# A two-layer decoder trunk: triangular inverse on 64x64 blocks, threshold search on keys with a sign per row, and the second layer's first loads ahead of a loop

## The chip, the cores and the metric

The kernel runs on one core of a Trainium2 chip, as one program. The metric is the device time of one execution in microseconds (us), the median of several runs. TensorE is called PE below, with PEld for its weight loads; VectorE is DVE, ScalarE is ACT, GpSimd is POOL, and SyncE, whose queue issues most transfers, is SP.

## The reference

Two decoder layers run one after the other over 1024 tokens of width 1024. Each layer mixes tokens with four head groups (RWKV-7, stick-breaking attention, mLSTM, and a sparse attention DSA), and then runs a mixture of 32 experts. What matters here, cut down:

```python
# RWKV-7: a delta rule over time; the kernel works in chunks of 64 tokens,
# and within a chunk the rule becomes a triangular system (I - L) T = I
def step(state, inp):
    rt, wt, kt, vt, kkt, at = inp
    sa = jnp.einsum('bhvk,bhk->bhv', state, -kkt)
    state = (state * wt[:, :, None, :] + sa[..., None] * (kkt * at)[:, :, None, :]
             + vt[..., None] * kt[:, :, None, :])
    return state, jnp.einsum('bhvk,bhk->bhv', state, rt)

# DSA: each query keeps its 256 best keys
idx_score = jnp.where(adm, idx_score, -jnp.inf)
vals, sel = lax.top_k(idx_score, n_sel)

# experts: top 2 of 32, results added at the tokens' rows
x = x + gt2 * hier_moe(h, ...)
```

## The kernel before

**Stages.** Per layer: the normed input and the first columns of the input projection (the head: `head`, `hidden`, `proj_i`); a weave of the projection on PE with the search for the 256th best score of each row on DVE and ACT (`proj` and `select`, which calls `Dsa.search`); a weave of four streams (`rw.run()`, which is RWKV; `dsr()` and `rest()`, which are the attentions and mLSTM; `mods()`; `outs()`, the output projection), called stage 3 below; the routing; the experts, one after another, each with 12 pieces of 512 KB of weights read from HBM. After the experts `moe.overflow` runs a loop whose number of turns is read from memory; in layer 1 it turns no time in the profiled execution, in layer 2 once (3544 to 3597 us). A weave takes the streams' pieces by turns, and a scheduler then places each instruction in its engine's order, which is fixed when the program is built.

**RWKV.** `Rwkv.run` keeps up to three units alive; a unit is one pair of heads over 128 tokens, that is two chunks of 64 tokens in two heads. There are 16 units in a layer: five batches of three and one alone. A unit holds the tiles `ra`, `bkv`, `mp` and `tl`. In `unit` the inverse T of each chunk is built by doubling: a mask `lev` cuts a level out of the 64x64 triangle, and in five steps a product `pw` (PSUM pool `b`), its copy by ACT into `ra`, a product `pT` (PSUM pool `pj`) and an addition by DVE into `tl` double the size of the blocks that are done; T and its transpose are both kept. Before, the two chunks of a head stand on the diagonal of a 128x128 matrix whose other two quarters are zero, so each product is one 128x128x128 matmul per head. All matmuls here are float32, and each leaves two records in the trace.

**The search.** `Dsa.search` finds each row's threshold bit by bit, first 16 upper bits of the score as a bfloat16 key (`upper`), then 16 lower bits (`lower`). Six tiles of 128 rows, 384 to 1024 keys wide, form two groups of three that take turns; per bit and group one count runs on ACT (line 1022) and two on DVE (line 1024), and small DVE operations on a 128x3 tile then decide the bit.

**The queue at the layer boundary.** The second layer's first loads are issued by SP in program order behind the loop: eight pieces of `w_in` (`wr`), the norm's gain (`ng`), the modulation (`mod`), then the tokens' rows `x`, which the experts' last scatters into `xs` (POOL, line 1502) must have written.

Of the kernel before, what the change touches and what calls it, by code (L numbers as in the profile page):

```python
# [12 lines left out]
BF16 = mybir.dt.bfloat16  # L13
# [36 lines left out]
def const_table():  # L50
# [24 lines left out]
    lev = lambda b: (s // (2 * b) == t // (2 * b)) & (s % (2 * b) < b) & (t % (2 * b) >= b)  # L75
# [19 lines left out]
class K:  # L95


    def __init__(self, ctx, tc, nbig, nmed, consts_dram):
# [9 lines left out]
        t = self.big("lev", 768)  # L108
        self.nc.sync.dma_start(t, consts_dram[:, NCONST:NCONST + 768])
        self.lev = self.cp.tile([P, 768], BF16, name="levb")  # L110
# [134 lines left out]
class Rwkv:  # L245
# [109 lines left out]
    def unit(self, ct, hf, nb, own):  # L355
# [28 lines left out]
        ml, w1 = [two(w[:, 256 * i:256 * i + 256]) for i in range(2)], two(ra[:, 256:512])  # L384
        tt = w[:, 512:1024].rearrange("p (x h t) -> p x h t", x=2, h=2)
        l2 = mp[:, :, 0, :].unsqueeze(2).to_broadcast([P, 2, 2, 64])
        four = lambda x: x.rearrange("p h (c t) -> p h c t", c=2)
        lv = lambda i: k.lev[:, 128 * i:128 * i + 128].rearrange("p (c t) -> p c t", c=2).unsqueeze(1).to_broadcast([P, 2, 2, 64])
        V.tensor_tensor(four(tt[:, 1]), l2, lv(0), op=ALU.mult)
        V.tensor_tensor(tt[:, 1], tt[:, 1], k.c("ident").unsqueeze(1).to_broadcast([P, 2, P]), op=ALU.add)  # L390
        for i in range(2):
            G.tensor_tensor(four(ml[i]), l2, lv(i + 1), op=ALU.mult)

        def chunks(out, a, b):
# [10 lines left out]
        for i in range(5):  # L405
            last = i == 4
            pw = two(k.psum("b", 256))
            for h in range(2):
                k.mm(pw[:, h], ml[i % 2][:, h], tt[:, 0, h])
            k.act(w1, pw)  # L410
            if i < 3:
                G.tensor_tensor(four(ml[i % 2]), l2, lv(i + 3), op=ALU.mult)
            pT = k.psum("pj").rearrange("p (x h t) -> p x h t", x=2, h=2)
# [10 lines left out]
        chunks(pn, mp[:, :, 2, :], two(bkv[:, 2, :]))  # L424
# [82 lines left out]
    def run(self, width=3):  # L507
# [7 lines left out]
        free = [(k.med("ra"), k.med("bkv", 384), k.med("mp"), k.big("tl", 1024)) for _ in range(width)]  # L515
# [353 lines left out]
class Dsa:  # L869
# [122 lines left out]
    def search(self):  # L992
# [4 lines left out]

        k, nc = self.k, self.k.nc
# [4 lines left out]
        cnt, sg, tt, k1, ml, thr, half_n = (t[:, 6 * i:6 * i + 6] for i in range(7))  # L1003
# [10 lines left out]
        for j, i in enumerate(tiles):  # L1014
            V.memset(half_n[:, j:j + 1], width(i) / 2.0)

        def counts(keys, val, g):

            for j in range(3 * g, 3 * g + 3):
# [3 lines left out]
                else:  # L1023
                    V.tensor_scalar(junk[j % 3 - 1][:, :width(i)], keys[i], v, None, op0=ALU.is_ge, op1=ALU.add,  # L1024
# [1182 lines left out]
```

## Time and profile before

| | |
|---|---|
| median of 3 runs | 3617.0 us (3612.22 to 3620.91) |
| the profiled execution | 3611.5 us, span 3609.7 us |
| mean granted TensorE clock of it | 0.922 of full speed |
| PE, DVE, ACT, POOL busy | 88%, 77%, 53%, 25% of the span |
| stage 3, layer 1 and layer 2 | 445 to 1165 us and 2240 to 2895 us |
| experts, layer 1 and layer 2 | 1200 to 1812 us and 2927 to 3544 us |

The busy share of an engine is a mean over stages with different limits, so each stage has to be read by itself; a chain of waits says which work was late in it. The span is the time from the first to the last instruction, 1.8 us less than the execution's own time.

### The profile page before, as it was taken

How to read it: one execution, taken by the hardware profiler on the slowest of the kernel's cores; microseconds unless marked ns; L12 is line 12 of the kernel's file. 1: busy time of each engine (PE TensorE's matmuls, PEld its weight loads, DVE VectorE, ACT ScalarE, POOL GpSimd, SP SyncE). 2: the span in 40 equal slices, each digit the busy share in tenths (PEclk: the TensorE clock that was granted, in tenths of full speed). 3: DMA queues.
4: the chain of work that ended last, by engine and by line, in shares of the span. 5: the costliest groups of instructions: out<-in, count | busy, mean ns of one | idle time of the engine just before them, and what ended most of it. 6: DMA issues, size and time to landing. Idle time of an engine off the chain costs nothing.

```text
span 3609.7 us, 54562 instructions
## 1 busy us (share of the span) xinstructions
PE 3185.2 (88%) x18836; PEld 2491.4 (69%) x18848; DVE 2778.3 (77%) x5552; ACT 1928.5 (53%) x3324; POOL 900.9 (25%) x769
## 2 busy tenths in 40 slices
PE   6888989998888799999968888989888879999996
PEld 3876745576666677777758766767676667887775
DVE  4589854567776899999965898666677679999996
ACT  3456333334444567777753563542444456777774
POOL 3220110113322215522312201121332221353231
PEclk8988989999997899999989899989889879999998
DMA  5222365433434799999932233023343379999996
GB/s 199 77 86 88 107 217 203 162 128 106 135 115 149 276 366 386 381 381 382 385 114 66 85 94 105 29 71 122 106 141 121 128 257 371 381 381 382 384 382 225
DMA packets 373672, 746.63 MB, mean 207 GB/s; under 512 B 44234, under 2 KB 108384, under 8 KB 373392
## 3 DMA queue, kind: packets, MB, share of 16 engines
q1 hardware_dynamic: 346880, 672.03, 51.7%
q0 software_dynamic: 20256, 70.33, 7.5%
q8 instruction: 151, 2.47, 0.3%
q10 hardware_dynamic: 6256, 0.74, 0.1%
q14 instruction: 129, 1.06, 0.1%
HBM read 635.45 MB, written 107.53 MB: 206 GB/s over the span
## 4 chain that ended last, share of the span: by engine, by line
PE 47%; DVE 21%; DMA 18%; issue 7%; ACT 4%; POOL 2%; SPq 1%; ACTq 0%; DVEq 0%; POOLq 0%
PE pj L143 26%; PE b L143 14%; DMA wr<-in_moe_w_dram 11%; DVE dkey L1024 4%; PE a L143 3%; PE a L148 2%; DMA xs<-yo,si 2%; DVE wl L1535 2%; DVE e L589 1%; PE pj L148 1%; ACT wh L160 1%; PE b L148 1%; DVE h L1785 1%; DVE yo L1499 1%; DVE z L591 1%
## 5 line engine op out<-in xcount | busy, mean ns | idle before, releaser
L160 ACT ACTIVATE wh<-wr 128x1024 fp32r<-128x1024 f32 (+3 forms) x900 | 886.7, 1006 | 293.8 <-DMA wr<-in_moe_w_dram 111.5
L1535 DVE TENSOR_TENSOR wl<-wr,wh 128x1024 fp32r<-128x1024 f32 x792 | 935.5, 1220 | 55.9 <-ACT wh L160 45.4
L143 PE MATMUL pj<-wh,xh 128*128 128x512 f32 x1056 | 421.5, 400 | 11.2 <-ACT xh L160 9.2
L143 PE MATMUL pj<-wl,xh 128*128 128x512 f32 x1056 | 418.7, 403 | 13.7 <-DVE wl L1535 13.2
L143 PE MATMUL pj<-wh,xl 128*128 128x512 f32 x1056 | 419.8, 398 | 0.0
L143 PEld LDWEIGHTS pj<-wl,xh 128*128 128x128 f32 x1056 | 200.1, 189 | 81.2 <-DVE wl L1535 37.6
L143 PEld LDWEIGHTS pj<-wh,xh 128*128 128x128 f32 x1056 | 199.8, 190 | 58.1 <-ACT xh L160 11.8
L143 PEld LDWEIGHTS pj<-wh,xl 128*128 128x128 f32 x1056 | 200.4, 190 | 45.5 <-DVE xl L1547 1.0
L1431 POOL DMA_INDIRECT xg<-h2d,si x64 | 78.4, 1224 | 582.5 <-PE a L148 345.5
L143 PE MATMUL b<-wh,hh 128*128 128x512 f32 x528 | 210.5, 399 | 10.2 <-ACT wh L160 9.1
L143 PE MATMUL b<-wh,hl 128*128 128x512 f32 x528 | 208.1, 394 | 1.2 <-DVE hl L1547 1.2
L143 PE MATMUL pj<-hh,wh 128*128 128x512 f32 x480 | 196.6, 410 | 13.0 <-ACT wh L160 5.9
L143 PE MATMUL pj<-wh,hh 128*128 128x256 f32 (+2 forms) x640 | 187.8, 306 | 17.2 <-DVE stl L1977 11.0
L143 PE MATMUL pj<-hh,wl 128*128 128x512 f32 x480 | 195.3, 407 | 3.9 <-DVE wl L1860 3.9
L1502 POOL DMA_INDIRECT xs<-yo,si x32 | 164.1, 5127 | 134.0 <-DVE yo L1499 117.6
L143 PE MATMUL pj<-wh,hl 128*128 128x256 f32 (+2 forms) x640 | 192.9, 303 | 3.0 <-DVE hl L1837 2.8
L1502 POOL DMA_INDIRECT out_dram<-yo,si x32 | 160.9, 5027 | 134.1 <-DVE yo L1499 117.5
L143 PE MATMUL pj<-hl,wh 128*128 128x512 f32 x480 | 193.9, 404 | 0.0
L143 PE MATMUL pj<-wl,hh 128*128 128x256 f32 (+2 forms) x640 | 189.1, 298 | 2.7 <-POOL wl L1860 2.7
L143 PE MATMUL b<-wl,hh 128*128 128x512 f32 x528 | 174.7, 410 | 2.3 <-DVE wl L1535 2.1
L160 ACT ACTIVATE ra<-b 128x256 f32<-128x256 f32 x192 | 72.9, 383 | 187.8 <-PE b L143 185.1
L421 DVE TENSOR_TENSOR tl<-pj,tl 128x512 f32<-128x512 f32 x128 | 87.4, 686 | 80.7 <-PE pj L143 80.0
(524 smaller groups left out, 7725.7 us busy)
## 6 DMA issues: line engine op xcount, KB each, us to landing
wr<-in_moe_w_dram SPq DMA_DIRECT2D x792, 512.0 KB
aw<-in_ada_w_dram SPq DMA_DIRECT2D x96, 512.0 KB
wr<-in_w_in_dram SPq DMA_DIRECT2D x84, 256.0 KB
wo<-in_w_out_dram SPq DMA_DIRECT2D x48, 256.0 KB
xs<-xp SPq DMA_DIRECT2D x48, 256.0 KB
xp<-xs SPq DMA_DIRECT2D x48, 256.0 KB
out_dram<-xp SPq DMA_DIRECT2D x48, 256.0 KB
sk<-pt SPq DMA_DIRECT2D x32, 256.0 KB
```

What stands on the lines that cost most here:

```text
L143: return self.nc.tensor.matmul(out, lhsT, rhs, start=start, stop=stop, skip_group_check=True)
L148: return self.nc.tensor.transpose(out, in_, self.c("ident")[o:o + n, o:o + n])
L160: i = self.nc.scalar.activation(out, in_, f, **kw)
L421: V.tensor_tensor(tt, pT, tt, op=ALU.add)
L589: V.tensor_tensor_scan(e[:, :kl][:, ::-1], e[:, :kl][:, ::-1], e[:, :kl][:, ::-1], initial=0.0, op0=ALU.add, op1=ALU.bypass)
L591: V.tensor_tensor(z[:, :kl], z[:, :kl], e[:, :kl], op=ALU.subtract)
L1024: V.tensor_scalar(junk[j % 3 - 1][:, :width(i)], keys[i], v, None, op0=ALU.is_ge, op1=ALU.add, accum_out=cnt[:, j:j + 1])
L1431: i = self.k.nc.gpsimd.indirect_dma_start(out=xg, out_offset=None, in_=self.h2d, in_offset=bass.IndirectOffsetOnAxis(ap=gi.bitcast(U32), a ...
L1499: i = V.scalar_tensor_tensor(yo[:, ns], py[n], gate, gt2[:, ns], op0=ALU.mult, op1=ALU.mult)
L1502: k.nc.gpsimd.indirect_dma_start(out=self.xs, out_offset=bass.IndirectOffsetOnAxis(ap=si.bitcast(U32), axis=0), in_=yo, in_offset=None, co ...
L1535: i = nc.vector.tensor_tensor(wl, raw, wh.bitcast(F32), op=ALU.subtract)
L1785: V.scalar_tensor_tensor(hs[i], xs[i], ms[:, 2 + i:3 + i], s, op0=ALU.mult, op1=ALU.mult)
```

## The change

It has three parts. In `Rwkv.unit` the 128x128 matrices with two zero quarters become 64x64 blocks, one per chunk, so the work tile, the masks and the copies are half as wide, and each 128x128 matmul becomes two 64x64 ones. In `Dsa.search` the keys are multiplied by a sign `sg` per row as ACT casts them, the counts on DVE count what is below the threshold, and a limit `lim` per row takes the place of the conversions behind each count. In `run` and `head` the pieces of `w_in` of the second layer are fetched and split ahead of the overflow loop, and `head2` holds what stays behind it.

```diff
-        ml, w1 = [two(w[:, 256 * i:256 * i + 256]) for i in range(2)], two(ra[:, 256:512])
-        tt = w[:, 512:1024].rearrange("p (x h t) -> p x h t", x=2, h=2)
+        ml, w1 = [two(w[:, 128 * i:128 * i + 128]) for i in range(2)], two(ra[:, 256:384])
+        tt = w[:, 256:512].rearrange("p (x h t) -> p x h t", x=2, h=2)
...
+        def chunks(*jobs):
             for h in range(2):
-                for c in ch:
-                    k.mm(out[c, h], a[c, h], b[c, h])
+                for out, a, b in jobs:
+                    for c in ch:
+                        k.mm(out[c, h], a[c, h], b[c, h])
-        pT = two(k.psum("b", 256))
+        pT = two(k.psum("b", 128))
         for h in range(2):
-            k.tr(pT[:, h], tt[:, 1, h])
+            for c in ch:
+                k.mm(pT[c, h], tt[c, 1, h], k.c("rep64")[c])
...
-            for h in range(2):
-                k.mm(pw[:, h], ml[i % 2][:, h], tt[:, 0, h])
+            chunks((pw, ml[i % 2], tt[:, 0]))
...
-            for h in range(2):
-                if not last:
-                    k.mm(pT[:, 0, h], tt[:, 1, h], w1[:, h])
-                k.mm(pT[:, 1, h], w1[:, h], tt[:, 1, h])
+            chunks(*[(pT[:, 0], tt[:, 1], w1)] * (not last), (pT[:, 1], w1, tt[:, 1]))
...
-        for h in range(2):
-            k.mm(pu[:, h], tt[:, 1, h], rh[:, h].rearrange("p x c -> p (x c)"))
+        chunks((pu, tt[:, 1], two(ra[:, 0:256])))
...
-                    V.tensor_scalar(junk[j % 3 - 1][:, :width(i)], keys[i], v, None, op0=ALU.is_ge, op1=ALU.add,
+                    V.tensor_scalar(junk[j % 3 - 1][:, :width(i)], keys[i], v, None, op0=ALU.is_lt, op1=ALU.add,
...
-        for i in tiles:
-            k.act(key[i], half[i][:, :, 1])
...
+        for j, i in enumerate(tiles):
+            k.act(key[i], half[i][:, :, 1], scale=sg[:, j:j + 1])
...
-                fix(g)
-                yield
-                V.scalar_tensor_tensor(tt[:, s], cnt[:, s], 0.5 - TOPK, sg[:, s], op0=ALU.add, op1=ALU.mult)
-                yield
                 if bit > 15:
-                    V.tensor_scalar(k1[:, s], tt[:, s], 0.0, float(1 << bit), op0=ALU.is_ge, op1=ALU.mult)
+                    V.tensor_tensor(k1[:, s], cnt[:, s], lim[:, s], op=ALU.is_le)
                     yield
-                    V.tensor_tensor(m[:, s], m[:, s], k1[:, s], op=ALU.add)
+                    V.scalar_tensor_tensor(m[:, s], k1[:, s], float(1 << bit), m[:, s], op0=ALU.mult, op1=ALU.add)
...
+        if l + 1 < L_LAYERS:
+            self.head(l + 1)
         moe.overflow(gt2)
```

On PE, one step of one unit of the first batch in layer 1, before. `b` is the product `pw` or a copy, `pj` the product `pT`, `tl` and `ra` the unit's tiles; `pj<-aw,cz` belongs to `mods()`, `dz`, `dat` and `dsum` to `dsr()`.

```order
L143 MATMUL b_4858<-tl_4463 128x128 x2
L143 MATMUL b_4915<-tl_4455 128x128 x2
L143 MATMUL pj_4836<-aw_4837,cz 32x512 x2
L148 MATMUL pj_4846<-cst,dz_4802 128x128 x3
L143 MATMUL pj_4863<-ra_4460,tl_4463 128x128
L143 MATMUL pj_4863<-tl_4463,ra_4460 128x128
L143 MATMUL pj_4863<-ra_4460,tl_4463 128x128
L143 MATMUL pj_4863<-tl_4463,ra_4460 128x128
L143 MATMUL pj_4836<-aw_4839,cz 32x512 x2
L143 MATMUL b_4851<-dat_4845,dv_325 64x128
```

The same place in the changed kernel:

```order
L143 MATMUL b_4777<-tl_4346 64x64 x4
L143 MATMUL pj_4720<-aw_4721,cz 32x512 x2
L148 MATMUL pj_4730<-cst,dz_4697 128x128 x3
L143 MATMUL pj_4742<-ra_4339,tl_4342 64x64 x2
L143 MATMUL pj_4742<-tl_4342,ra_4339 64x64 x2
L143 MATMUL pj_4742<-ra_4339,tl_4342 64x64 x2
L143 MATMUL pj_4742<-tl_4342,ra_4339 64x64 x2
L143 MATMUL pj_4720<-aw_4723,cz 32x512 x2
L143 MATMUL b_4752<-dat_4729,dv_325 64x128
```

The two 128x128 matmuls of `pw` became four 64x64 ones and the four of `pT` eight, in the same neighbourhood: matmuls of other streams, on the whole array or on parts of another shape, stand between the groups as before.

On DVE, one upper bit of both groups of the search in layer 1, before: line 1058 makes the thresholds, 1024 counts, 1041 to 1070 decide.

```order
L1058 TENSOR_SCALAR dmi_2213<-dmi_2213 128x3
L1024 TENSOR_SCALAR dkey_2215,dth_2212<-dkey_2215,dmi_2213 128x768
L1024 TENSOR_SCALAR dkey_2216,dth_2212<-dkey_2215,dmi_2213 128x512
L1041 SCALAR_TENSOR_TENSOR dth_2212<-dth_2212 128x1
L1065 SCALAR_TENSOR_TENSOR dth_2212<-dth_2212 128x3
L1068 TENSOR_SCALAR dth_2212<-dth_2212 128x3
L1041 SCALAR_TENSOR_TENSOR dth_2212<-dth_2212 128x1
L1070 TENSOR_TENSOR dmi_2213<-dmi_2213,dth_2212 128x3
L1065 SCALAR_TENSOR_TENSOR dth_2212<-dth_2212 128x3
L1058 TENSOR_SCALAR dmi_2213<-dmi_2213 128x3
L1068 TENSOR_SCALAR dth_2212<-dth_2212 128x3
L1024 TENSOR_SCALAR dkey_2215,dth_2212<-dkey_2214,dmi_2213 128x640
```

In the changed kernel, where line 1056 makes the thresholds, 1022 counts, and 1062 and 1064 decide:

```order
L1056 TENSOR_SCALAR dmi_2213<-dmi_2213 128x3
L1022 TENSOR_SCALAR dkey_2215,dth_2212<-dkey_2215,dmi_2213 128x768
L1022 TENSOR_SCALAR dkey_2216,dth_2212<-dkey_2215,dmi_2213 128x512
L1062 TENSOR_TENSOR dth_2212<-dth_2212 128x3
L1064 SCALAR_TENSOR_TENSOR dmi_2213<-dth_2212,dmi_2213 128x3
L1056 TENSOR_SCALAR dmi_2213<-dmi_2213 128x3
L1022 TENSOR_SCALAR dkey_2215,dth_2212<-dkey_2214,dmi_2213 128x640
```

Per group and bit three small operations are left of five, and here they stand one behind another, where before those of the two groups alternated.

On POOL, at the end of layer 1's experts, in the changed kernel (before, the two scatters into `xs` stand next to each other, and the splits `wl` behind the loop):

```order
L1497 DMA xs_80<-yo_17233,si_11302 1152x1024
L1863 TENSOR_TENSOR wl_17309<-wr_17292,wh_17308 128x292
L1863 TENSOR_TENSOR wl_17313<-wr_17294,wh_17312 128x292
L1863 TENSOR_TENSOR wl_17317<-wr_17296,wh_17316 128x292
L1863 TENSOR_TENSOR wl_17321<-wr_17298,wh_17320 128x292
L1863 TENSOR_TENSOR wl_17325<-wr_17300,wh_17324 128x292
L1863 TENSOR_TENSOR wl_17329<-wr_17302,wh_17328 128x292
L1863 TENSOR_TENSOR wl_17333<-wr_17304,wh_17332 128x292
L1497 DMA xs_80<-yo_17288,si_11302 1152x1024
```

Seven of the eight splits moved in front of the last scatter. On SP, behind the loop, the changed kernel issues two pieces of `x` first, then `ng`, `mod` and the others; the eight `wr` stand ahead of the loop.

## Rows read from the trace of the kernel before

**Rows 1.** Windows by stage: projection and search, stage 3, experts.
```profile
core 0: us, PE busy (x) PEld busy (x) DVE busy (x) ACT busy (x) POOL busy (x), PEclk, DMA share, GB/s
200.00:445.00 245.00, 218.46 (x1046) 178.53 (x1046) 229.04 (x741) 130.51 (x237) 36.04 (x48) 0.91 0.32 98
445.00:1165.00 720.00, 636.32 (x4779) 446.95 (x4781) 445.83 (x949) 276.07 (x657) 156.05 (x199) 0.91 0.45 151
1200.00:1812.00 612.00, 591.17 (x2699) 470.65 (x2699) 564.80 (x631) 453.27 (x508) 196.85 (x59) 0.99 1.02 371
2240.00:2895.00 655.00, 571.55 (x4490) 446.34 (x4495) 443.77 (x947) 276.83 (x660) 157.14 (x195) 0.89 0.32 103
```

**Rows 2.** Chain of waits by line, stage 3 of layer 2.
```profile
by line: PE b L143 24.4%; PE pj L143 23.6%; PE a L143 8.2%; issue 5.8%; DVE e L589 3.7%; PE pj L148 3.2%; PE a L148 3.1%; DVE z L591 1.7%; DVE wol L2096 1.3%; DMA sk<-pt 1.2%; ACT e L160 1.1%; DMA wo<-in_w_out_dram 1.1%; DVE tl L421 1.0%; A
```

**Rows 3.** Windows of the twelve stretches with inverse steps, all tiles; columns as above.
```profile
871.00:920.00 49.00, 47.45 (x366) 39.98 (x366) 36.79 (x65) 22.16 (x55) 16.44 (x26) 1.00 0.38 131
...
2378.00:2449.00 71.00, 61.14 (x411) 48.74 (x414) 39.77 (x86) 22.03 (x60) 12.77 (x17) 0.83 0.14 43
...
sum 661.00, PE 585.42 PEld 458.66 DVE 440.24 ACT 264.07 POOL 167.32; mean PE 48.79 PEld 38.22 DVE 36.69 ACT 22.01 POOL 13.94
```

**Rows 4.** The same windows, instructions of tile tl alone.
```profile
sum 661.00, PE 287.12 PEld 250.74 DVE 101.55 ACT 11.53 POOL 72.67; mean PE 23.93 PEld 20.90 DVE 8.46 ACT 0.96 POOL 6.06
```

**Rows 5.** Timeline: start us, us, engine, line, operation; 128x128 matmuls of `pT`.
```profile
706.38 0.39 PE L143 MATMUL pj<-tl,ra 128*128 128x128 f32 x2
...
706.60 0.39 PE L143 MATMUL pj<-ra,tl 128*128 128x128 f32 x2
```

**Rows 6.** Timeline: chunk matmuls of 64x64 between 128x128 ones.
```profile
712.82 0.61 PE L143 MATMUL pj<-tl,ra 128*128 128x128 f32 x4
713.36 0.45 PE L143 MATMUL b<-bkv,mp 64*64 64x64 f32 x8
...
713.74 0.71 PE L143 MATMUL pj<-tl,ra 128*128 128x128 f32 x4
```

**Rows 7.** Groups by form, layer 1: additions of `tl`, duration ns min/median/max.
```profile
L421 DVE TENSOR_TENSOR tl<-pj,tl x64: 637/692/693, 498.4 to 1069.0; 128x512 f32<-128x512 f32 x64
...
L419 DVE TENSOR_TENSOR tl<-pj,tl x16: 414/422/425, 563.3 to 1072.8; 128x256 f32<-128x256 f32 x16
```

**Rows 8.** Groups by form, layer 1: the counts on DVE.
```profile
L1024 DVE TENSOR_SCALAR_CACHE_REDUCE dkey<-dkey,dmi x64: 603/812/1015, 220.5 to 294.1; 128x640 bf16<-128x640 bf16 x16, 128x384 bf16<-128x384 bf16 x16, 128x768 bf16<-128x768 bf16 x16, 128x512 bf16<-128x512 bf16 x16
...
L1024 DVE TENSOR_SCALAR_CACHE_REDUCE dkey<-dkey,dth x64: 606/808/1015, 300.1 to 376.1; 128x640 bf16<-128x640 uint16 x16, 128x384 bf16<-128x384 uint16 x16, 128x768 bf16<-128x768 uint16 x16, 128x512 bf16<-128x512 uint16 x16
```

**Rows 9.** Timeline of DVE in the search: one upper bit.
```profile
268.37 0.88 DVE L1024 TENSOR_SCALAR_CACHE_REDUCE dkey<-dkey,dmi 128x640 bf16<-128x640 bf16 x1
...
271.51 0.16 DVE L1041 SCALAR_TENSOR_TENSOR dth<-dth 128x1 f32<-128x1 f32 x1
271.70 0.17 DVE L1065 SCALAR_TENSOR_TENSOR dth<-dth 128x3 f32<-128x3 f32 x1
...
272.51 0.88 DVE L1024 TENSOR_SCALAR_CACHE_REDUCE dkey<-dkey,dmi 128x640 bf16<-128x640 bf16 x1
```

**Rows 10.** Chain of waits in time, projection and search: start us, us.
```profile
336.71 47.05 PE pj L143 x191
```

**Rows 11.** Timeline at the layer boundary.
```profile
1812.82 2.28 POOL L1502 DMA_INDIRECT xs<-yo,si  x1 [7.00 <-DVE yo L1499]
...
1820.38 1.55 POOL L1502 DMA_INDIRECT xs<-yo,si  x1 [5.28 <-DVEq L1402]
1827.34 3.66 SPq L1849 DMA_DIRECT2D wr<-in_w_in_dram  x8
...
1830.09 6.13 POOL L1860 TENSOR_TENSOR wl<-wr,wh 128x292 fp32r<-128x292 f32 x8 [8.16 <-DMA wr<-in_w_in_dram]
...
1831.99 3.59 SPq L1790 DMA_DIRECT2D x<-xs  x4
...
1840.74 1.06 ACT L160 ACTIVATE h<-x 128x1024 f32<-128x1024 f32 x1 [5.73 <-DMA x<-xs]
```

More of the change, by code (lines that the diff above doesn't have):

```diff
@@ L107, in __init__ @@
         self.nc.sync.dma_start(self.cst, consts_dram[:, 0:NCONST])
-        t = self.big("lev", 768)
-        self.nc.sync.dma_start(t, consts_dram[:, NCONST:NCONST + 768])
-        self.lev = self.cp.tile([P, 768], BF16, name="levb")
+        t = self.med("lev", 384)
+        self.nc.sync.dma_start(t, consts_dram[:, NCONST:NCONST + 384])
+        self.lev = self.cp.tile([P, 384], BF16, name="levb")
         self.nc.vector.tensor_copy(self.lev, t)
@@ L406, in unit @@
             last = i == 4
[L407 to L409 removed]
+            pw = two(k.psum("b", 128))
+            chunks((pw, ml[i % 2], tt[:, 0]))
             k.act(w1, pw)
             if i < 3:
[L412 to L417 removed]
+                G.tensor_tensor(ml[i % 2], l2, lv(i + 3), op=ALU.mult)
+            pT = k.psum("pj", 256).rearrange("p (x h t) -> p x h t", x=2, h=2)
+            chunks(*[(pT[:, 0], tt[:, 1], w1)] * (not last), (pT[:, 1], w1, tt[:, 1]))
             if last:
@@ L423, in unit @@
         pn = two(k.psum("b", 128))
-        chunks(pn, mp[:, :, 2, :], two(bkv[:, 2, :]))
+        chunks((pn, mp[:, :, 2, :], two(bkv[:, 2, :])))
         V.tensor_copy(rh[:, :, 1, :], pn)
         pu = two(k.psum("b", 256))
-        for h in range(2):
-            k.mm(pu[:, h], tt[:, 1, h], rh[:, h].rearrange("p x c -> p (x c)"))
+        chunks((pu, tt[:, 1], two(ra[:, 0:256])))
         k.act(au.rearrange("p h x c -> p h (x c)"), pu)
@@ L514, in run @@
         k = self.k
-        free = [(k.med("ra"), k.med("bkv", 384), k.med("mp"), k.big("tl", 1024)) for _ in range(width)]
+        free = [(k.med("ra"), k.med("bkv", 384), k.med("mp"), k.med("tl")) for _ in range(width)]
         while units or live or side:
@@ L1002, in search @@
         t = k.small("dth", 54, bufs=1)
-        cnt, sg, tt, k1, ml, thr, half_n = (t[:, 6 * i:6 * i + 6] for i in range(7))
+        cnt, sg, lim, k1, ml, thr, num = (t[:, 6 * i:6 * i + 6] for i in range(7))
         mi = k.small("dmi", 18, bufs=1, dt=I32)
@@ L1014, in search @@
         for j, i in enumerate(tiles):
-            V.memset(half_n[:, j:j + 1], width(i) / 2.0)
+            V.memset(num[:, j:j + 1], float(width(i)))
         def counts(keys, val, g):
@@ L1087, in lower @@
                 yield from counts(low, thr, g)
[L1088 removed]
+                V.tensor_tensor(k1[:, s], cnt[:, s], lim[:, s], op=ALU.is_le)
                 yield
[L1090 to L1094 removed]
+                V.scalar_tensor_tensor(ml[:, s], k1[:, s], float(1 << bit), ml[:, s], op0=ALU.mult, op1=ALU.add)
                 yield
@@ L1804, in head, with head2 @@
         nc.vector.tensor_copy(self.sh, p)
+    def head2(self, l):
+        k, nc = self.k, self.nc
+        self.x += [self.x_tile(l, i) for i in range(len(self.x), 2)]
+        if l:
+            self.s1 = self.scale_of(l, 1, "norm1_g")
+        self.x += [self.x_tile(l, i) for i in range(2, 4)]
         self.rope = [k.med("rope"), k.med("rope", 256)]
@@ L1807, in head @@
         nc.sync.dma_start(self.rope[1], self.ins["rope"][:, 512:768])
-        self.x += [self.x_tile(l, i) for i in range(len(self.x), 4)]
         self.small_weights(l)
```

45 lines of the change are left out of this document (23 added, 22 removed).

## Prediction

> **What bounds the kernel now.** I read the windows by stage first, since the busy share of the whole span mixes stages with different limits [rows 1]. The experts are a transfer stage: their DMA share is 1.02 at 371 GB/s, and nothing of the change lies inside them, so they only move. In stage 3 PE is busy 636 of 720 us in layer 1 and 572 of 655 us in layer 2, at a granted clock of 0.91 and 0.89, and DVE 446 and 444. The chain of waits of layer 2's stretch names PE on 62.5% (24.4 + 23.6 + 8.2 + 3.2 + 3.1), with no line of another engine above 4% [rows 2]. So stage 3 is mostly PE's, and a PE microsecond saved there is worth about 0.65. In projection and search DVE is busy 229 of 245 us. The counts run from 220.5 to 376 us [rows 8], but the chain lies on 191 matmuls in a row for 47 us, from 336.7 on [rows 10]: PE takes over as the bound before the bits are done.
>
> Where do the inverse steps lie? Twelve stretches, 661 us in all, hold them; PE is busy 585 us (88.6%) there [rows 3], and with instructions of tile `tl` alone 287 us [rows 4].
>
> **The inverse on PE.** In a group of `pT` a 128x128 matmul (two records) starts every 0.22 us: 706.38, 706.60 [rows 5]. A unit has 30 of these and two transposes of one record: 30 x 0.224 + 0.224 = 6.94 us. For 64x64 blocks the nearest row is `pn`, which is already done by chunks: eight records from 713.36, and the next group starts at 713.74, 0.38 us later [rows 6]. In front of it, four records of 128x128 from 712.82 took 0.54 us to that start, where their own pace, 0.112 each, gives 0.45, so some 0.09 us went at the change of shape. Splitting the rest is my estimate: two chunks work in different quarters of the array at once, a pair takes 0.116 us, so four matmuls take 0.232 of the 0.38, and 0.15 us goes at the change back. A visit to the other shape thus costs 0.24 us, each change 0.12. A unit after has 60 matmuls of 64 columns (60 x 0.058 = 3.48) and four of 128, at twice that (4 x 0.116 = 0.46): 3.94 us. Sixteen units save 16 x 3.00 = 48 us per layer. Counting changes of shape along PE's order in stage 3 gives 495 before and 593 after in layer 1, and 387 and 496 in layer 2: 98 and 109 more, at 0.12 us 12 and 13 us. What is left is -36 and -35 us. At 0.65 on the chain that is **-47 us** for both layers. Bounds: from -18, where a quarter passes, to -72, where all does.
>
> The Trainium skill bears on this in TensorEngine Tiling (Array Packing), Performance Considerations: a change of the tiling mode, not merely of the tile, drains the engine. It speaks against the change, and rows 6 agree: about 0.24 us for a visit. By the rows alone an isolated `pw` would go from 0.448 to 0.47 us, no gain, and only the longer `pT` group gains, from 0.90 to 8 x 0.058 + 0.24 = 0.70. If each of a unit's twelve groups were isolated, the visits would cost 12 x 0.24 = 2.9 us of the 3.0 that it saves, which is a rival below; 98 more changes in 16 units are only three visits per unit, so most groups share a neighbour.
>
> **Its elementwise part.** The addition in `tl` goes from 128x512 (692 ns) to 128x256, for which another line has 422 [rows 7]; four of these and one of half that size per unit, and two first operations, make some 1.8 us of DVE per unit, 29 us per layer. ACT's copies and POOL's masks halve too. Most of it lies beside PE: `tl` on DVE holds 1.0% of layer 2's chain [rows 2], 6.6 us, of which four tenths would go. It counts in full only where one unit runs alone at the end of a layer, with some 0.4 us in each of five steps. I take -4 per layer, **-8 us**, bounds 0 and -24. The tile `tl` goes from the big buffers to the medium ones, three of each; that asks for no transfer and I cost it at nothing.
>
> **The search.** One bit of both groups takes 4.14 us, 268.37 to 272.51; the last count ends at 271.51 and ten small operations (one of them ahead of the second group's counts) fill about 1.2 us, 0.12 each [rows 9]. Six are left. Where they alternate between groups they start 0.1 us apart; behind an operation that they need, 0.19 (271.51 to 271.70). At 0.12 four of them save 0.48 per bit, 15 us over 32 bits; if all six wait for each other, 6 x 0.2 = 1.2, nothing is saved. Walking the order of DVE with these two gaps gives 147 us of bits before (156 measured) and 136 after, so I take -11.7 per layer. ACT's casts now wait for the signs, where before they stood ahead of the first counts. A cast of such a width is no shorter than a count, 0.6 to 1.0 us [rows 8], and two to three stand ahead of the first bit: 1 to 3 us, of which the first counts give some back, since they wait for no cast. I take 1. What follows is PE's, 47 us of it unbroken [rows 10], and PE is idle 27 of the 245 us [rows 1], so an earlier search helps it only in part; I take 0.65 here too. That is -7 per layer, **-14 us**, bounds 0 and -24.
>
> **The loop and the first loads.** SP issues eight `wr` in 3.66 us from 1827.34; the first `x` goes out at 1831.99, and ACT starts its norm at 1840.74 after 5.7 us of waiting for `x` [rows 11]. After the change `x` leaves at 1827.34, 4.7 us earlier, and 1.2 MB of `wr` no longer shares the queues with it. `ng` and `mod` leave behind two `x` instead of behind `wr`, some 2.7 us earlier, and are then late next. I take **-6 us**; the bounds are -3 and -8. Seven splits of `wl` now stand on POOL before the last scatter, at 6.13 us for eight [rows 11]. The scatter before it, 2.28 us from 1812.82, leaves POOL at 1815.1, so the splits end near 1820.5, where the scatter started at 1820.38: this costs next to nothing while the weights arrive by then, and if they are late it moves the scatter and all behind it by as much. SP's own loads go in front of the loop, behind the last weights of the experts, whose transfers have ended.
>
> **The sum.** -47 - 8 - 14 - 6 = -75. Against the profiled execution, 3611.5 us, that is 3536.5; the median of the runs shown is 5.5 us above that execution, so I expect **3542 us**.
>
> **Rivals.** *The shape changes eat the gain* (chance 0.2). The place is each `pw` group that stands alone between other shapes. For it: an isolated `pw` gains nothing by rows 6. Against it: the counts above. If only a quarter of the PE time reaches the end, -18, with half of search, -6, and -5 at the boundary: -29, 3588 us.
>
> *Everything passes* (0.1). PE's 72 us in full, 16 elementwise, 24 in the search, 8 at the boundary and a few at the end of layer 2, where the lone unit starts earlier in PE's order: -125, 3492 us. Against it is that a third of the chain is other engines' [rows 2].
>
> *The clock falls* (0.08), the rival on the slower side. In the stretches of rows 3, 871 to 920 us has PE busy for 47.45 of 49 us and a granted clock of 1.00, and 2378 to 2449 has 61.14 of 71 and 0.83. The change takes PE work out of streams that stay as long on DVE and ACT, so PE's busy share of stage 3 falls, by my sum from 88% (1208 of 1375 us) to 86% (1137 of 1320). The 1137 us of PE work that remain grow with the ratio of the clocks. Drawn between the two rows, two points are 0.03 of clock; a fall from 0.90 to 0.87 costs 39 us of PE, 25 of time: 3567. The gain is gone when it costs 114 us of PE, at 0.82. At 0.80 it costs 142 us of PE, 92 of time, and the kernel takes 3634 us. Against it: the fall would have to be almost three times what the rows suggest.
>
> *The blocks do not run in pairs* (0.04): the two chunks go one after the other, a matmul keeps 0.116 us, a unit needs as much as before and the changes of shape come on top: +25 us of PE, +16 of time, with -14 and -6 from the other parts and the narrower elementwise work -8: about 3605. Rows 6 speak against it.
>
> **How the numbers follow.** The forecast has 0.58, its own range 3515 to 3570. The range for 8 in 10 reaches to the first rival and most of the second: 3495 to 3602. A measurement of this kernel tells some 0.2% from no change, 7 us: faster by more than that 0.85, within it 0.06 (the pairs, or the clock near 0.82), slower 0.09.
>
> **What would show it.** Right: in stage 3 PE's busy time falls by 30 us or more per layer while its share of the chain falls little; `pT` groups of 64x64 take 0.7 us alone and 0.46 among their like; the bits take some 144 us instead of 156; ACT's norm in layer 2 starts 12 to 17 us after the last scatter instead of 20. Wrong: a stage 3 as long as before with more idle time on PE, which is the first rival, or a clock under 0.85 there; POOL's last scatter more than 2 us behind DVE's last `yo`, with `wr` as its releaser.

## The result and the profile after

The changed kernel takes 3574.0 us (median; 3567.3 to 3582.4), the kernel before in the same comparison 3614.6 us: ratio 0.9886, 95% interval 0.9871 to 0.9901, a gain of 41 us. Single executions of one kernel spread by 15 us and more, so a profiled one can lie well off its median; where it does, its own time is given. The forecast was 3542 us with a range of 3495 to 3602: the right side, inside the range, and 32 us short of the likeliest case.

The windows of the changed kernel's profiled execution (span 3570.7 us), for projection and search, stage 3 of layer 1, the experts, and stage 3 of layer 2; columns as in [rows 1]:

```profile
200.00:440.00 240.00, 211.22 (x1031) 172.90 (x1031) 216.67 (x624) 134.66 (x241) 32.66 (x48) 0.91 0.32 98
440.00:1147.00 707.00, 614.34 (x5856) 411.83 (x5855) 417.66 (x955) 265.06 (x657) 130.32 (x199) 0.88 0.46 155
1182.00:1794.00 612.00, 590.46 (x2701) 470.88 (x2701) 565.47 (x632) 454.12 (x509) 191.82 (x60) 0.99 1.03 373
2211.00:2853.00 642.00, 550.74 (x5557) 412.76 (x5556) 409.83 (x952) 267.51 (x660) 128.69 (x195) 0.86 0.33 105
```

Stage 3 went from 720 to 707 us and from 655 to 642 [rows 1]: 26 us of the 41. PE is busy 22 us less in layer 1 (636.32 to 614.34) and 21 less in layer 2, where I had expected 36 and 35; my sign of being right, 30 us or more per layer, did not appear. The clock column says why: 0.91 became 0.88, and 0.89 became 0.86. PE's busy time times the granted clock is roughly its work at full clock: 636.32 x 0.91 = 579 against 614.34 x 0.88 = 541, and 571.55 x 0.89 = 509 against 550.74 x 0.86 = 474. So the work fell by 38 and 35 us, as the sum had it, and two fifths of that were given back by the clock. The column is rounded, which is worth some 3 us in each product; with the clock that the trace records for each moment in which PE was busy, the work goes from 587 to 550 us and from 512 to 475, 36 and 37 us less. The experts are as they were: 612 us, at the same transfer rate.

One `pT` group of 64x64 blocks among others, in the timeline of PE (start us, duration us, instruction, number of records):

```profile
514.11 0.33 PE L143 MATMUL pj<-ra,tl 64*64 64x64 f32 x4
514.28 0.28 PE L143 MATMUL pj<-tl,ra 64*64 64x64 f32 x4
514.39 0.28 PE L143 MATMUL pj<-ra,tl 64*64 64x64 f32 x4
514.51 0.28 PE L143 MATMUL pj<-tl,ra 64*64 64x64 f32 x4
514.72 0.70 PE L143 MATMUL b<-sqh,cst 128*128 128x512 f32 x1
```

The sixteen records of eight products go from 514.11 to the next shape at 514.72, 0.61 us with the change back; with 0.09 for the change in front that is the 0.70 of my sum, against 0.90 before. DVE's addition behind it took 423 ns, as the row of the half-sized form had said [rows 7]:

```profile
L418 DVE TENSOR_TENSOR tl<-pj,tl x64: 391/423/426, 496.3 to 1061.8; 128x256 f32<-128x256 f32 x64
```

The search's counts on DVE in layer 1:

```profile
L1022 DVE TENSOR_SCALAR_CACHE_REDUCE dkey<-dkey,dmi x64: 606/812/1014, 222.5 to 288.6; 128x640 bf16<-128x640 bf16 x16, 128x384 bf16<-128x384 bf16 x16, 128x768 bf16<-128x768 bf16 x16, 128x512 bf16<-128x512 bf16 x16
...
L1022 DVE TENSOR_SCALAR_CACHE_REDUCE dkey<-dkey,dth x64: 606/805/1014, 295.4 to 364.2; 128x640 bf16<-128x640 uint16 x16, 128x384 bf16<-128x384 uint16 x16, 128x768 bf16<-128x768 uint16 x16, 128x512 bf16<-128x512 uint16 x16
```

The bits run from 222.5 to 364.9 us, 142 us against 156 [rows 8]; in layer 2 they take 143 us against 155. One bit of both groups, in the timeline of DVE:

```profile
261.78 0.88 DVE L1022 TENSOR_SCALAR_CACHE_REDUCE dkey<-dkey,dmi 128x640 bf16<-128x640 bf16 x1
...
265.12 0.15 DVE L1064 SCALAR_TENSOR_TENSOR dmi<-dth,dmi 128x3 int32<-128x3 f32 x1
265.31 0.17 DVE L1056 TENSOR_SCALAR dmi<-dmi 128x3 int32<-128x3 int32 x1
265.39 0.15 DVE L1062 TENSOR_TENSOR dth<-dth 128x3 f32<-128x3 f32 x1
265.51 0.88 DVE L1022 TENSOR_SCALAR_CACHE_REDUCE dkey<-dkey,dmi 128x640 bf16<-128x640 bf16 x1
```

From 261.78 to 265.51 it is 3.73 us, before 4.14 [rows 9]; of the three small operations between the counts, the two of one group (lines 1064 and 1056) stand 0.19 us apart, and the third (line 1062) belongs to the other group.

At the layer boundary, the last four splits of expert weights on DVE before the change:

```profile
1812.46 4.62 DVE L1535 TENSOR_TENSOR wl<-wr,wh 128x1024 fp32r<-128x1024 f32 x4
```

In the changed kernel DVE, then POOL, then ACT:

```profile
1795.69 7.90 DVE L1530 TENSOR_TENSOR wl<-wr,wh 128x1024 fp32r<-128x1024 f32 x2
1804.48 1.41 DVE L1494 SCALAR_TENSOR_TENSOR yo<-b,sf,mod 128x512 f32<-128x512 f32 x2 [0.89 <-PE b L143]
```
```profile
1796.58 5.92 POOL L1863 TENSOR_TENSOR wl<-wr,wh 128x292 fp32r<-128x292 f32 x7
1806.17 1.55 POOL L1497 DMA_INDIRECT xs<-yo,si  x1 [3.67 <-DVEq L1397]
```
```profile
1816.56 1.06 ACT L160 ACTIVATE h<-x 128x1024 f32<-128x1024 f32 x1 [2.09 <-DMA x<-xs]
```

PE's first matmul of layer 2, before and then in the changed kernel:

```profile
1845.89 0.69 PE L148 MATMUL a<-cst,h 128*128 128x128 f32 x2 [17.68 <-DVE h L1785]
```
```profile
1824.36 0.69 PE L148 MATMUL a<-cst,h 128*128 128x128 f32 x2 [19.49 <-DMA rope<-in_rope_dram]
```

ACT's norm starts 10.4 us after the last scatter (1806.17 to 1816.56), before 20.4 [rows 11]. Less of that reaches PE: its first matmul comes 18.2 us after the scatter, before 25.5, so 7 of the 10 us. And the scatter itself is late. Two of DVE's last splits of expert weights take 7.90 us together, where four took 4.62 before (1.22 each, a little overlapped); they lie beside the seven splits of `w_in` that POOL does from 1796.58 on. The last `yo` and the scatter wait for them, so some 5 of the 7 us are lost ahead of the loop.

### The profile page after: what moved, and what is told of

Its sections match the earlier page's. It is cut to its first block, busy times and chain, and to the rows that moved or that the text cites. A ratio compares the mean times of both kernels' runs of the same rounds, so it can differ in the third digit from the quotient of the medians.

```text
span 3570.7 us, 58618 instructions
## 1 busy us (share of the span) xinstructions
PE 3122.1 (87%) x20960; PEld 2407.3 (67%) x20960; DVE 2696.4 (76%) x5318; ACT 1913.5 (54%) x3324; POOL 821.6 (23%) x769
## 4 chain that ended last, share of the span: by engine, by line
PE 50%; DVE 20%; DMA 18%; issue 5%; ACT 5%; POOL 1%; SPq 0%; ACTq 0%; DVEq 0%; POOLq 0%
PE pj L143 27%; PE b L143 14%; DMA wr<-in_moe_w_dram 11%; DVE dkey L1022 5%; PE a L143 4%; PE a L148 3%; DMA xs<-yo,si 3%; PE pj L148 1%; DVE wl L1530 1%; DVE e L585 1%; ACT wh L160 1%; DVE h L1780 1%; PE b L148 1%; ACT e L160 1%; DVE z L587 1%
## 5 line engine op out<-in xcount | busy, mean ns | idle before, releaser
L1497 POOL DMA_INDIRECT out_dram<-yo,si x32 | 148.3, 4633 | 135.3 <-DVE yo L1494 120.9
L160 ACT ACTIVATE ra<-b 128x128 f32<-128x128 f32 (+1 forms) x192 | 54.3, 293 | 165.5 <-PE b L143 163.8
L143 PEld LDWEIGHTS pj<-wh,hh 128*128 128x128 f32 x640 | 121.7, 195 | 18.2 <-ACT st L160 6.4
```

Source lines behind the costliest of these rows:

```text
L143: return self.nc.tensor.matmul(out, lhsT, rhs, start=start, stop=stop, skip_group_check=True)
L160: i = self.nc.scalar.activation(out, in_, f, **kw)
L1497: k.nc.gpsimd.indirect_dma_start(out=self.xs, out_offset=bass.IndirectOffsetOnAxis(ap=si.bitcast(U32), axis=0), in_=yo, in_offset=None, co ...
```

## The experiments

Each is timed against the kernel before, on the same chip. Ratios carry their 95% interval. My theory, theory 1 of the expectations on the inverse, was that PE's work fell as forecast and that the granted clock fell with it, since the shorter products leave PE idle for more of the stretch; each expectation names the rival that it is set against, and numbers its theories by itself.

**One part at a time.** The first kernel has the hunks of `Rwkv`, `run` and the masks alone, the second those of `Dsa.search`, the third those of `head`, `head2` and `run`.

> Only the triangular inverse on 64x64 blocks. Theory 1 (the clock): PE's work at equal clock falls by about 40 us per layer in stage 3, but the granted clock of stage 3 falls from 0.91 and 0.89 to about 0.88 and 0.86, so PE busy falls by only some 22 us per layer, and the kernel gains 25 to 30 us (ratio 0.992). Theory 2 (the changes of shape eat the gain): the clock stays at 0.91 and 0.89, PE busy still falls by only 20 us, same total. Theory 3 (the parts help each other): alone it gains under 15 us, since the earlier search is what lets stage 3 use the freed time. The clock in stage 3 tells 1 from 2, the total tells 3.

> Only the search with negated rows. Theory 1: the bits take 142 us instead of 156 in each layer, 4 to 7 us of the 14 reach the start of stage 3 because PE bounds the end of the projection, and the kernel gains 9 to 13 us (ratio 0.997). Rival: stage 3 gives these back, since its order of work was as late at its end as before; then the gain is under 4 us, with the same 142 us of bits.

> Only the first loads ahead of the loop. Theory 1: ACT's first norm of layer 2 starts 12 to 15 us after the last scatter into xs instead of 20, a gain of 6 to 9 us behind the scatter, but the scatter itself is 5 us late, because the last DVE split of the experts takes about 6.8 us instead of 1.2 while POOL's seven splits run beside it. Total gain 1 to 5 us, within what can be told from nothing. Rival: the scatter is late because it stands behind the splits on POOL; then the last DVE split takes 1.2 us as before and DVE's last yo is not late.

The inverse alone takes 3587.5 us, ratio 0.9924 (0.9911 to 0.9938), 28 us; the search alone 3607.9 us, 0.9980 (0.9970 to 0.9990), 7 us; the loads alone 3616.1 us, 0.9996 (0.9985 to 1.0007), nothing that can be told. Together that is 35 of 41 us, the whole within the intervals, so the parts do not need each other, and theory 3 falls. Stage 3 of the inverse alone, by windows:

```profile
448.00:1164.00 716.00, 621.19 (x5846) 419.62 (x5839) 419.51 (x949) 264.47 (x658) 128.07 (x199) 0.87 0.45 152
2240.00:2884.00 644.00, 554.91 (x5550) 413.82 (x5548) 410.54 (x947) 267.67 (x660) 131.03 (x195) 0.85 0.33 105
```

The clock is 0.87 and 0.85, PE's busy time 15 and 17 us below that of before: theory 1 and not theory 2, which asked for an unchanged clock. The profiled execution took 3603.4 us.

For the search alone the counts show the full saving in the bits, 223.7 to 366.2 us:

```profile
L1026 DVE TENSOR_SCALAR_CACHE_REDUCE dkey<-dkey,dmi x64: 606/811/1015, 223.7 to 289.8; 128x640 bf16<-128x640 bf16 x16, 128x384 bf16<-128x384 bf16 x16, 128x768 bf16<-128x768 bf16 x16, 128x512 bf16<-128x512 bf16 x16
...
L1026 DVE TENSOR_SCALAR_CACHE_REDUCE dkey<-dkey,dth x64: 605/810/1014, 296.6 to 365.5; 128x640 bf16<-128x640 uint16 x16, 128x384 bf16<-128x384 uint16 x16, 128x768 bf16<-128x768 uint16 x16, 128x512 bf16<-128x512 uint16 x16
```

Some 14 us are saved in layer 1 and 12 in layer 2, and 7 us of both together arrive. PE sets the end of the projection: from the first count to its last matmul the traces have 223.9 and 222.8 us before and 217.8 and 218.3 here, so 6 and 4.5 us reach the start of stage 3. Whether stage 3 gives part of these back is not shown, since the interval (4 to 11 us) holds the 9 of the theory and touches the 4 of its rival.

For the loads alone, DVE and POOL at the boundary:

```profile
1820.96 7.90 DVE L1535 TENSOR_TENSOR wl<-wr,wh 128x1024 fp32r<-128x1024 f32 x2
1831.17 1.41 DVE L1499 SCALAR_TENSOR_TENSOR yo<-b,sf,mod 128x512 f32<-128x512 f32 x2 [2.31 <-PE b L143]
```
```profile
1820.71 5.92 POOL L1868 TENSOR_TENSOR wl<-wr,wh 128x292 fp32r<-128x292 f32 x7
1832.86 1.55 POOL L1502 DMA_INDIRECT xs<-yo,si  x1 [6.23 <-DVEq L1402]
```

The same 7.90 us stand in DVE's row beside the same splits on POOL, without the other two parts. DVE's last `yo` is late itself, so POOL's order alone, the rival, is not the cause. The scatter at 1832.86 is some 6 us late (11.9 us behind the first of the two splits, before 5.7), and PE's first matmul of layer 2 follows it by 18.8 us in place of 25.5: the one takes what the other gives.

**The splits behind the loop.** The whole change, with the eight casts and splits moved from `head` to `head2`:

```diff
-        self.wi = self.split(self.fetch(l, D0 + 256, 292), 292, nc.gpsimd)
+        raws = self.fetch(l, D0 + 256, 292)
+        if l == 0:
+            self.wi = self.split(raws, 292, nc.gpsimd)
+        else:
+            self.raws = raws
...
         self.x += [self.x_tile(l, i) for i in range(2, 4)]
+        if l:
+            self.wi = self.split(self.raws, 292, nc.gpsimd)
```

> The whole change, but with the casts and splits of the eight pieces of w_in left behind the loop; their loads stay ahead. Theory 1 (DVE is held up while POOL's splits run): the last DVE split of the experts is back at 1.2 us, the last scatter starts some 5 us earlier than in the changed kernel, ACT's norm starts as soon after it as there (10 us), perhaps 1 to 2 us later for casts in between, and the kernel takes 3 to 5 us less than the changed kernel (some 3569 us). Rival (only POOL's order delays the scatter): same total, but the DVE split was not the cause and stays long.

DVE's last two splits of the experts, and ACT behind the loop:

```profile
1804.94 2.35 DVE L1530 TENSOR_TENSOR wl<-wr,wh 128x1024 fp32r<-128x1024 f32 x2
1808.58 1.41 DVE L1494 SCALAR_TENSOR_TENSOR yo<-b,sf,mod 128x512 f32<-128x512 f32 x2 [1.29 <-PE b L143]
```
```profile
1819.44 0.45 ACT L160 ACTIVATE wh<-wr 128x292 fp32r<-128x292 f32 x1 [16.78 <-DMA xs<-yo,si]
...
1821.20 0.78 ACT L160 ACTIVATE wh<-wr 128x292 fp32r<-128x292 f32 x2
1822.47 1.06 ACT L160 ACTIVATE h<-x 128x1024 f32<-128x1024 f32 x1 [0.49 <-DMA x<-xs]
```

Both splits are back at 1.2 us each (2.35 together), and `yo` follows 1.3 us later: POOL's splits had held DVE up. The Trainium skill states the mechanism in SBUF — State Buffer, Who interferes with whom: a DVE instruction with two inputs in SBUF contends with a POOL instruction that reads SBUF, since its second input comes through a read interface that the two engines share, and the shared ports are held exclusively. The rows agree, and they show that DVE's split stayed blocked over the whole row of seven POOL instructions.

The time is 3575.4 us, ratio 0.9893 (0.9876 to 0.9911), not to be told from the changed kernel's 0.9886. Three casts now stand ahead of ACT's norm, which still starts 10.8 us after the scatter (1811.64). Counted from the first of the two splits, PE's first matmul of layer 2 comes after 26.1 us, in the changed kernel after 28.7. The expected 3 to 5 us were not found in the time; they are at the edge of what these runs resolve.

**The shapes by themselves.** The changed kernel with a stretch of matmuls at its start whose results go nowhere; the kernel's time is not compared. `whole` issues 128x128 products, `waits` the same in groups with a wait for DVE between them, `pairs` two 64x64 products, `mixed` four of each by turns, `narrow` 32-column ones.

```diff
+        def pairs(p, x, n):
+            for _ in range(n):
+                for c in ch:
+                    k.mm(p[c, 0:64], rep[c], x[c, 0:64])
...
+        for f, args in ((whole, (300,)), (waits, (24, 10)), (whole, (200,)), (waits, (8, 25)), (whole, (200,)),
+                        (pairs, (600,)), (whole, (200,)), (mixed, (40,)), (whole, (200,)), (narrow, (30,)), (whole, (100,))):
```

> The changed kernel with a stretch of matmuls by themselves put at its start, whose results go nowhere (its time is not compared): whole 128x128 matmuls without a wait; whole ones in groups of 24 and of 8 with a wait for DVE between groups; pairs of 64x64 in two quarters without a wait; four whole ones and four pairs by turns; 32-column matmuls of 512. Theory 1 (idle time lowers the clock): pairs without a wait keep a granted clock of 1.00, groups with a wait fall below it, the groups of 8 lower than those of 24. Theory 2 (the small shape lowers it): the pairs fall below 1.00 with PE busy throughout. Prices: a whole matmul 0.224 us, a pair 0.116 us, a visit to the other shape 0.24 us, so a turn of four and four takes 0.90 + 0.46 + 0.24 = 1.60 us; if a change of shape costs more than I took, the turn is longer.

By windows: groups of 8 whole matmuls with short waits; the first 6 us behind a long wait; pairs of 64x64 without a wait; four whole ones and four pairs by turns. Then the row of the timeline at which the long wait ends:

```profile
200.00:249.00 49.00, 41.35 (x325) 37.54 (x325) 5.82 (x20) 4.94 (x11) 6.85 (x9) 1.00 0.07 27
254.00:260.00 6.00, 5.55 (x26) 5.58 (x27) 0.90 (x3) 0.00 (x0) 0.00 (x0) 0.50 0.45 112
...
303.00:372.00 69.00, 69.00 (x2374) 69.00 (x2372) 0.22 (x4) 0.00 (x0) 0.00 (x0) 1.00 0.02 5
419.00:487.00 68.00, 67.67 (x959) 60.10 (x958) 0.23 (x1) 0.00 (x0) 0.00 (x0) 1.00 0.01 2
```
```profile
254.45 1.83 PE L143 MATMUL a<-prb,cst 128*128 128x128 f32 x7 [4.88 <-DVE prb L2223]
```

The pairs keep a clock of 1.00 for 69 us, so the small shape by itself does not lower it: theory 2 falls. Theory 1 as I had put it falls too. The groups of 8 leave PE idle in 7.65 of 49 us, in waits of 0.38 us, a larger share than stage 3 has, and the clock stays at 1.00; so it does with the groups of 24 and the 32-column products. What was followed by a clock of 0.50 was the one long wait, 4.88 us ahead of 254.45. So the idle share of a stretch by itself did not tell its clock here.

The pairs run at 0.117 us (600 in 70 us), as taken. A turn takes 1.70 us (40 in 68 us); less 0.90 and 0.47 a visit to the other shape costs 0.34 us, not the 0.24 that I had split from rows 6. At 98 and 109 more changes that would be 5 us per layer more than I took off. In the kernel itself it is not seen: the group of eight products above took 0.61 us to the next shape, as the 0.24 has it, so the dearer visit is shown for this sequence of shapes alone.

**Every product twice.** In `chunks` of the changed kernel each product is issued again over the first, in the same group:

```diff
                     for c in ch:
                         k.mm(out[c, h], a[c, h], b[c, h])
+                    for c in ch:
+                        nc.tensor.matmul(out[c, h], a[c, h], b[c, h], start=True, stop=True, skip_group_check=True)
```

> The changed kernel with every 64x64 product of the inverse's steps issued twice, the second over the first, in the same group, so that no change of shape is added: per unit 60 more of 64 columns and 4 of 128, 3.95 us at full clock, 126 us of PE for both layers. The step of my sum that is tested is that a microsecond of PE in stage 3 is worth 0.65: then the time rises by about 80 us over the changed kernel, to 3655, at an unchanged clock. If the saved PE work had turned into waits that cost clock (theory 1), the added work fills waits and the clock rises again, to 0.92 or more, so the rise is smaller, 45 to 65 us. If PE's time in the inverse is not on the path (rival), under 30 us.

```profile
443.00:1191.00 748.00, 667.12 (x7898) 470.81 (x7903) 414.23 (x954) 265.02 (x657) 130.94 (x199) 0.92 0.44 146
2258.00:2945.00 687.00, 605.06 (x7599) 470.90 (x7605) 411.60 (x952) 266.96 (x660) 131.07 (x195) 0.88 0.31 99
```

The time is 3667.4 us, ratio 1.0154 (1.0125 to 1.0183), 93 us over the changed kernel for 126 us of PE: 0.74 per microsecond. So PE's time in the inverse is on the path at this order of the streams, and the 0.65 of the sum was low rather than high. The clock comes back to 0.92 and 0.88 in the two stages, and to 0.923 over the kernel in the median of its runs (0.9145 for the changed kernel). More work for PE in the same places raised its clock: that is the change run backwards. The rise in time met neither number: it was above the 80 us of the 0.65, and above the 45 to 65 of theory 1, whose clock came true.

**The order of the streams.** RWKV's pace in the weave of stage 3 is 260; a smaller number lets it take fewer turns.

```diff
-        weave(k, [(rw.run(), 260)], [(dsr(), 350), (rest(), 140)], [(mods(), 550)], [(outs(), 150)])
+        weave(k, [(rw.run(), 300)], [(dsr(), 350), (rest(), 140)], [(mods(), 550)], [(outs(), 150)])
```

> The changed kernel with RWKV's stream of the stage 3 weave at pace 300 instead of 260, so that its units stand earlier in PE's order (the last unit of layer 1 by about 110 rows). Theory 1 (the clock, set by idle time, holds the rest of the gain): the end of layer 1's stage 3 waits less for the last unit, but the granted clock stays near 0.915 and the gain over the changed kernel is under 10 us. Rival (the lone last unit's chain of waits holds it): the changed kernel had streams 30 us ahead while the last RWKV unit stood still, so with this stage 3 ends 10 us earlier in layer 1 and the kernel gains 10 to 15 us.

> As the run with pace 300, with pace 340 (the last unit about 210 rows earlier in PE's order). By the rival a further gain, 3550 to 3562 us in all; by theory 1 no more than the first step gives, and if RWKV then runs out of work before the attention does, more idle time at the end, a lower clock and a time above 3574 us.

> Pace 340 together with the casts and splits left behind the loop. If the two act apart from each other: the time of the run with pace 340 less 0 to 4 us. The last DVE split of layer 1's experts takes 1.2 us.

> The changed kernel with RWKV's pace 240 instead of 260: its last unit stands some 40 rows later in PE's order, behind the last matmuls of the attention's units, in both layers. The faster paces cost 55 and 89 us, with longer waits of PE and clocks of 0.905 and 0.897. If what counts is that RWKV's matmuls fill the attention's waits up to the end, this gains: 3555 to 3570 us at a clock of 0.92. If 260 is already the balance and each way costs, 3580 to 3600 us.

> Pace 250, half of that step. If the time follows the pace smoothly, it lies between 3574 us and that of pace 240; if the scheduler's order jumps, it need not, and a spread of over 20 us between 240, 250 and 260 would mean that such a part of the change's own result is the luck of the order rather than the work saved.

At 240, 250, 300 and 340 the changed kernel takes 3621.1, 3612.1, 3629.2 and 3662.7 us: against the kernel before ratios 1.0025 (1.0011 to 1.0039), 0.9999 (0.9985 to 1.0013), 1.0040 (1.0023 to 1.0057) and 1.0145 (1.0123 to 1.0168), and 1.0134 (1.0115 to 1.0153) at 340 with the splits behind the loop, where the last DVE split takes 1.22 us in place of 6.77. I had read from the trace that the last RWKV unit of layer 1 stood still while other streams ran 30 us ahead, and that giving it turns would help. All my expectations of a gain were wrong, and 3621 us at 240 is outside both ranges that I had given. 260 is the best of the five, and the step to 250 costs 38 us; the median clocks over the kernel are 0.908, 0.908, 0.905 and 0.895. Between 240, 250 and 260 the times spread by 47 us, more than the 20 that I had set as the sign that part of the change's result is the luck of the order. So the last test was of the change itself at another pace:

> The kernel before, with RWKV's pace 250 instead of 260. The changed kernel loses 38 us by this step. If the saved work is worth some 40 us in any order (theory 1), the kernel before at 250 takes about 3650 us, since both meet the same order of streams. If the order's luck is as large as the change itself, the two differ by something else than 41 us at 250: a kernel before that stays at 3614 us would mean that at this pace the whole change is worth nothing, and that the 41 us at pace 260 hold for that order alone.

The kernel before at pace 250 takes 3629.7 us, 1.0037 (1.0026 to 1.0049): neither the 3650 nor the 3614. The change is worth 3629.7 - 3612.1 = 18 us there, or 14 by the two ratios, less than half of the 41 at 260. Stage 3 of both at 250 by windows, the kernel before (an execution of 3639.9 us) and then the changed one (3627.3 us):

```profile
451.00:1177.00 726.00, 638.22 (x4785) 452.85 (x4785) 441.65 (x948) 273.96 (x657) 152.25 (x197) 0.91 0.46 150
2256.00:2920.00 664.00, 569.31 (x4486) 447.96 (x4485) 438.08 (x946) 276.67 (x660) 149.03 (x195) 0.88 0.32 101
```
```profile
444.00:1171.00 727.00, 633.18 (x5850) 424.27 (x5854) 411.67 (x955) 264.55 (x657) 134.69 (x199) 0.86 0.45 150
2241.00:2906.00 665.00, 564.65 (x5549) 423.41 (x5552) 410.12 (x951) 266.56 (x660) 136.08 (x195) 0.83 0.33 101
```

Stage 3 is as long with the change as without it, 727 and 665 against 726 and 664 us. The clock falls by 0.05 in each layer. PE's work at full clock still fell, from 638.22 x 0.91 = 581 to 633.18 x 0.86 = 545, and from 501 to 469: 36 and 32 us, as at pace 260 (33 and 37 by the recorded clock). So in these two executions the inverse gained no time in stage 3. Of the 13 us between them 11 lie in the two projections, which end earlier behind the first count (224.0 to 218.0 us and 223.1 to 218.1), and that is the search. The kernel before was timed at 250 and 260 alone.

## Why the prediction was right, and where it was short

**The inverse on PE.** The mechanism and the size of the saved work were right: 38 and 35 us at full clock, 36 and 32 at another pace, against 36 and 35 in the sum. The dearer visits (0.34 us) would make it 31 and 30; the rounded column cannot tell these apart, but the recorded clock (36 and 37) fits the sum. Two slips in it are small: 71 us at 0.65 are 46, not 47, and the visits are not three more per unit. In the traces 64x64 is entered 104 times before and 210 times after in stage 3 of layer 1, and 98 and 195 times in layer 2, six to seven more per unit.

**The step that fell short** is the price of that work in time: "At 0.65 on the chain that is -47 us" takes the clock of before for the work that remains. I had the other figure in the text, as part of a rival: two points of busy share, drawn between two rows, gave a fall of 0.03 and 25 us back, 3567 us. The clock fell by just that in both layers, and 3574 us came out; that the two times lie so near is in part luck, since the search and the loads fell some 13 us short as well. The fall belonged into the sum and stood beside it, since I used the rival's size only to ask whether the change could end slower. The line behind the figure, busy share against clock, did not hold elsewhere: the groups of 8 were at 1.00 with more idle time, and at pace 250 the fall was 0.05. So the right side and a time inside the range owe something to the order of the streams at pace 260: at 250 the same change gave 14 to 18 us.

How much time the clock took can be estimated from the runs. Within one kernel the longer runs are those with the lower mean clock: before, 3605.2 us at 0.925 and 3624.0 at 0.919; changed, 3567.3 at 0.916 and 3582.4 at 0.911; both pairs 3 us per thousandth. Lines through all runs of a kernel have slopes from 1.9 (the 71 runs of the kernel before) to 3.8. The medians of the runs' clocks are 0.922 and 0.9145, so 7.5 thousandths are some 22 us, 14 to 28 by that range: at equal clock the gain would be about 63 us. The same sum for the inverse alone (0.913) gives 28 + 27 = 55, and for the change at pace 250 (0.923 to 0.908) 18 + 45 = 63. Less the 7 us of the search that is 55 to 56 us for the inverse each time, and my -47 and -8 were 55. This agreement is closer than the slope allows, and one run speaks against it: the doubled products, whose clock rose by 8.5 thousandths, would by the same sum cost 93 + 26 = 119 us at equal clock for 126 us of PE, well above 0.65. So it is an estimate from a correlation, not a measurement at a held clock, which no run here could make; the doubled products speak for its direction.

Which waits does the clock answer to? PE's waits for the inverse's own tiles in stage 3 of layer 1, the kernel before and then the changed one (us in total, times, longest):

```profile
PE pj L143 <- ACT ra L160: 3.5, 5, 1.3
PE b L143 <- DVE tl L421: 3.5, 4, 1.8
```
```profile
PE pj L143 <- ACT ra L160: 7.7, 10, 2.1
PE b L143 <- DVE tl L418: 6.6, 3, 3.5
...
PE b L143 <- DVE tl L416: 4.8, 1, 4.8
...
PE b L143 <- DVE tl L389: 3.2, 1, 3.2
```

Waits of PE for `ra` and `tl` grew from 7 to 22 us, while PE's whole idle time in the stage grew from 84 to 93, so other waits shrank; in layer 2 the idle time grew from 83 to 91. One reading is that the products are shorter, ACT's copy and DVE's addition between them are shorter by less, and what stood between two steps of a unit as cover takes the same turns. It was argued, not tested, and the clock's record in the traces does not bear it out throughout. The time that the clock stood at 0.50 in stage 3 goes from 126 to 160 us in layer 1 and from 143 to 174 in layer 2. Sorted by the longest wait of PE just ahead of each fall, the part behind waits for `ra` or `tl` goes from 10 to 41 us and from 27 to 34; at pace 250 in layer 1 it goes from 24 to 14, while the time at 0.50 goes from 133 to 195. Which of the waits lower the clock, and why another order costs 38 us, stays open: the order moves everything at once.

**The elementwise part** has its durations right (423 ns against 422 taken); its -8 us cannot be told apart from the rest.

**The search.** -14 us forecast, -7 (4 to 11) measured. The saving in the bits was a little larger than taken, 14 and 12 us against 11.7; what was mis-sized is the 0.65 that should arrive: 10.5 of 26 us reach the end of the projections, and 7 the kernel's time, a quarter. The stage's chain lay on PE for 47 us without a break before the search ended [rows 10], which was to be weighted heavier than the idle time of PE.

**The loads.** -6 us forecast, nothing measurable alone. The gain behind the scatter was 10 us at ACT's norm, more than the sign I had given (12 to 17 us after the scatter), and 7 at PE's first matmul. I had priced the splits ahead of the scatter as POOL's time in POOL's queue, which was right (they ended at 1802.5, ahead of `yo`), and not what they do to DVE beside them, which took 5 to 6 us.

**The rivals.** The clock's fall happened, at three eighths of the size that would have decided the sign at 0.82; in stage 3 of layer 2 at pace 250 (0.83) it came close to it, and there stage 3 gained nothing. The blocks did run in pairs. The first rival, shape changes that eat the gain, holds at most to the part of 5 us per layer, which the kernel's own work does not show. The sentence on the drain that the prediction takes from TensorEngine Tiling (Array Packing) in the Trainium skill stands there under Key Properties.

## What to carry to other kernels

Work taken from PE is worth its time at the clock that it leaves behind, here 0.03 to 0.05 lower: put the expected fall into the sum, and read busy time together with the granted clock, since the busy time alone hid here two fifths of what was saved. Where several streams share an in-order engine, a change of one stream's costs is also a change of the order's fit; time both kernels at a second setting of the order before the difference is called the worth of the change. When work moves to an idle engine, look at what its neighbour does in the same microseconds, and not only at the queue that it joins.

## What the runs showed of the hardware

A DVE subtraction with two inputs in SBUF took 6.8 us instead of 1.22 while POOL ran seven subtractions one behind another (7.90 us for two in the changed kernel and in the loads alone, 2.35 with the splits moved): it did not get in between two of POOL's. Waits of PE of 0.38 us each, 16% of a 49 us stretch, left the granted clock at 1.00, and one wait of 4.88 us was followed by 0.50. Two 64x64 products on the two diagonal blocks ran side by side, 0.117 us a pair. A change between 128x128 and 64x64 products and back cost 0.34 us where the two shapes took turns. In stage 3 products half as long lowered the mean granted clock (0.91 to 0.88 and 0.89 to 0.86), and issuing them twice raised it again (0.92 and 0.88).
